# Regrouping the fp32 matrix work of a first stage: one place per row tile, the modulation a tile further ahead

## The chip, the cores and the metric

The kernel runs on one core of a Trainium2 chip. The metric is the device time of one launch in microseconds (us). Before the change it is 1366.4 us, the median of three runs (1366.26 to 1366.55).

The engines are TensorE (PE in the profile, its weight loads PEld), VectorE (DVE), ScalarE (ACT), GpSimd (POOL) and SyncE (SP, which here issues loads). Each works through its own instructions in order; between engines, semaphores make one wait for another.

## The reference

One layer of a hybrid decoder trunk over 1024 rows of 1024 numbers, all in float32. What matters here is its head:

```python
def rms_norm(x, w):
    xf = x.astype(jnp.float32)
    y = xf * lax.rsqrt(jnp.mean(xf * xf, axis=-1, keepdims=True) + EPS)
    return (y * w.astype(jnp.float32)).astype(x.dtype)

def hybrid_layer(x, c, ada_w, ada_b, norm_w, w_in, ...):
    mod = jax.nn.silu(c) @ ada_w + ada_b
    shift, scale, gate = jnp.split(mod, 3, axis=-1)
    h = rms_norm(x, norm_w) * (1 + scale[:, None, :]) + shift[:, None, :]
    proj = h @ w_in
    gm_u, gm_v, gm_z, ssm_z, xbc, dt_raw, g_a, g_b = jnp.split(proj, SPLITS, axis=-1)
    ...
    return x + gate[:, None, :] * (merged @ w_out)
```

The rest (a gated mixer over chunks, a state-space scan, two projections merged by gates, a last norm) follows the head and is not touched.

## The kernel before, in words

The first stage makes h, transposed so that its 1024 columns lie on the partitions, in eight row tiles of 128. It takes them in the order `KS = (0, 4, 1, 5, 2, 6, 3, 7)`; "tile n" below is the n-th in this order. Each tile has two halves of 512 columns (`halves(n)` says which comes first, a or b). What is done for a tile:

- `load_aw(n)`: SP loads the tile's part of `ada_w` (two transfers of 512 KB) into `aw`, which has two buffers; `load_w0(n)`: SP loads a slice of `w_in` into `w0r`.
- `matvec(n)`: eight fp32 matmuls, silu(c) times that part of `ada_w`, into `pm` (PSUM); ScalarE copies the result into `row`.
- `modulation_product(n)` ("the product"): two fp32 matmuls with a moving operand of one column, which sum the copied row over its four parts and turn it onto the partitions, in `pm` again.
- `modulation(n)`: two small instructions on VectorE that make the factors `md` from `pm`.
- `transposes(n, h)`: four fp32 matmuls against the identity, x to `px`.
- `rows_of_h(n, h)`: ScalarE writes h twice from `px` and `md`, once rounded to fp32r (the high part, such as `b22h`) and once in full (`hf`); VectorE makes the low part (such as `b22l`) as their difference.
- `split_w0(n)`: the same split into high and low for the weights.
- `first_products(n)`: twelve fp32r products into the accumulators `acc`: for each half, high times high, low weight times high, high weight times low.
- `dt_products(k)`: after every second tile, four fp32 matmuls of 32 columns into `pd`.
- `t_sum(k, i)` and `t_part(k, nm)`: four sums of h on VectorE (i from 0 to 3), and their splits on ScalarE and VectorE, for products by a Strassen-like scheme in later stages.

The order of all this on every engine is written by hand: `pin` keeps the instructions in the order of the program. The loop at the stage's end runs `first_products(n)`, a generator that gives way after each product, and puts the work for tile n+1 between the products of tile n: `prepare(n + 1)` says after which product, `between` adds the splits of the sums. In the stage after the first, TensorE runs the products `vx` and `vy`, whose weights SP loads into `av`.

Of the kernel before, what the change touches and what calls it, by code (L numbers as in the profile page):

```python
# [16 lines left out]
P = 128  # L17
D = 1024
S = 1024
KT = D // P  # L20
# [15 lines left out]
def hybrid_kernel(  # L36
# [7 lines left out]
    V, A, G, PE = nc.vector, nc.scalar, nc.gpsimd, nc.tensor  # L44
# [26 lines left out]
    def cst(shape, name, dt=F32):  # L71
        return const.tile(shape, dt, name=name, tag=name)
# [6 lines left out]
    pin = tc.keep_in_program_order  # L79

    def mm(acc, l, r, first=True, last=True):
        pin(PE.matmul(acc, l, r, start=first, stop=last))  # L82

    def tp(dst, src, idn):
        pin(PE.transpose(dst, src, idn))  # L85

    def f32(t):
        return t.bitcast(F32)

    def load(dst, src):  # L90
        pin(nc.sync.dma_start(dst, src))
# [6 lines left out]
    ones = cst([P, P], "ones")  # L98
# [16 lines left out]
    par = cst([P, P], "par")  # L115
# [27 lines left out]
    KS = (0, 4, 1, 5, 2, 6, 3, 7)  # L143
# [6 lines left out]
    def ax(name, tag="pm"):  # L150
        return psum0.tile([P, 512], F32, name=name, tag=tag, bufs=2 if tag == "px" else 1)
# [17 lines left out]
    def wide(name, dt=F32):  # L169
        return w4[0].tile([P, S], dt, name=name, tag="w4", bufs=w4[1])  # L170


    with tc.tile_pool(name="p0", bufs=1, reuse_waits="tile") as p0:
# [4 lines left out]
        accs = [[t[:, 0:512], t[:, 512:1024]] for t in accw]  # L178
        xt = [p0.tile([P, D], F32, name=f"x{t}", tag=f"x{t}") for t in range(NCH)]
        aw, wk = {}, {}  # L180
        pms, mds, hhs = {}, {}, {}

        def aw_tile(n):
            return p0.tile([P, KT, 2, P], F32, name=f"aw{n}", tag="aw", bufs=2)
# [56 lines left out]
        def warm(n):  # L241

            for _ in range(n):
                mm(pd[:, 0:P], ident, ones)

        tp(pp[:, 0:P], pk, ident)
        pin(V.tensor_copy(par, pp[:, 0:P]))
        warm(36)
        pin(V.tensor_scalar_add(par[:, 24:32], par[:, 24:32], 1.0))
        pin(A.activation(sc, par[:, 0:8], AF.Tanh, scale=0.5))  # L250
# [3 lines left out]

        def matvec(n):

            pms[n] = pm = ax(f"pm{n}")
            for i in range(KT):
                q = i % 4
                mm(pm[32 * q : 32 * q + 32, 0:256], scz[:, i, :], aw[n][:, i].rearrange("p j c -> p (j c)"),  # L260
                   i < 4, i >= 4)
            row = p0.tile([P, 256], F32, name=f"row{n}", tag="row", bufs=2)
            pin(A.copy(row, pm[:, 0:256]))
            mds[n] = row

        def modulation_product(n):

            pm, row = pms[n], mds[n]
            for j in range(2):
                mm(pm[:, 256 + j : 257 + j], row[:, j * P : (j + 1) * P], ones[:, 0:1])  # L270

        def modulation(n):

            k, pm = KS[n], pms[n]
            md = p0.tile([P, 2], F32, name=f"md{n}", tag="md", bufs=3)
            pin(V.tensor_add(md[:, 0:1], pm[:, 256:257], par[:, 16 + k : 17 + k]))
            pin(V.scalar_tensor_tensor(md[:, 1:2], pm[:, 257:258], par[:, 24 + k : 25 + k], par[:, 8 + k : 9 + k],
                                       op0=ALU.add, op1=ALU.mult))
            mds[n] = md

        def transposes(n, h):
            k = KS[n]
            px = pxs[n, h] if n + h == 0 else ax(f"px{n}_{h}", "px")
            for i in range(4):
                tp(px[:, i * P : (i + 1) * P], xt[4 * h + i][:, k * P : (k + 1) * P], ident)
            pxs[n, h] = px

        def rows_of_h(n, h):
            k, md, px = KS[n], mds[n], pxs[n, h]
            if k < 4 and h:  # L290
                b12 = wide(f"b12_{k}", F32R)
                hh, hl = b12[:, 0:512], b12[:, 512:1024]
            else:
                nm = ("b11" if k < 4 else ("b21", "b22")[h])
                hh, hl = bop[nm][0][k % 4], bop[nm][1][k % 4]
            if n + h:
                hfs[k, h] = hf_tile(k, h)
            hf = hfs[k, h]
            if n + h:
                for t in (hh, hf):  # L300
                    pin(A.activation(t, px, AF.Identity, scale=md[:, 1:2], bias=md[:, 0:1]))
            else:
                pin(V.tensor_scalar(hf, px, md[:, 1:2], md[:, 0:1], op0=ALU.mult, op1=ALU.add))
                pin(V.tensor_copy(hh, hf))
            pin(V.tensor_sub(hl, hf, f32(hh)))
            hhs[n, h] = (hh, hl)
# [6 lines left out]
        def t_sum(k, i):  # L313

            b11, b12, b21, b22 = (hfs[k + 4 * (j // 2), j % 2] for j in range(4))
            a, b, c = ((b11, b12, b11), (b12, b22, b12), (b22, b22, b11), (b21, b21, b22))[i]
            pin(V.tensor_sub(a, b, c))
# [53 lines left out]
        transposes(0, 0)  # L371
        split_w0(0)
        matvec(0)
        load_aw(2)
        load_w0(2)
        late_loads()
# [19 lines left out]
        rows_of_h(0, 1)  # L396
        warm(2)
        matvec(1)
        split_w0(1)
        for _ in range(2):  # L400
            next(start)
# [8 lines left out]
        def prepare(n):  # L410

            a, b = halves(n)
            k = (n - 2) // 2

            def second():
                modulation_product(n)
                transposes(n, b)
                if n % 2 == 0:
                    dt_products(k)
                modulation(n)  # L420
                if n % 2:
                    t_sum(k, 3)
                rows_of_h(n, a)
                if n % 2 == 0:
                    t_sum(k, 0)
                rows_of_h(n, b)
                if n % 2:
                    t_part(k, "t3")
                    t_part(k, "t2")
                else:  # L430
                    t_sum(k, 1)

            if n == 2:
                return {
                    4: lambda: (transposes(1, 1), rows_of_h(1, 1), matvec(n)),
                    8: lambda: (transposes(n, a), second()),
                }
            return {2: lambda: (matvec(n), transposes(n, a)), 7: second}

        def between(n, at):  # L440

            if n == KT - 1 and at == 6:
                dt_products(3)
            elif at == 2 and n > 1:
                k = (n - 2) // 2
                if n % 2:
                    t_part(k, "t4")
                else:
                    t_part(k, "t1")
                    t_sum(k, 2)  # L450

        for n in range(1, KT):
            todo = prepare(n + 1) if n + 1 < KT else {}
            for at, _ in enumerate(first_products(n), 1):
                if at == 1 and n + 2 < KT:
                    load_aw(n + 2)
# [5 lines left out]
                between(n, at)  # L462


    wpool = tc.tile_pool(name="wpool", bufs=1, reuse_waits="tile")
# [1107 lines left out]
    while tasks or work or posts:  # L1573
# [3 lines left out]
        while posts:  # L1577
            p, q, sq = posts.pop(0)
# [462 lines left out]
```

## Time and profile before

| | |
|---|---|
| median of three runs | 1366.4 us |
| time of the profiled execution | 1369.39 us |
| its span, first to last instruction | 1367.4 us |
| TensorE busy | 1352.4 us (99%) |
| VectorE busy | 1047.6 us (77%) |
| ScalarE busy | 799.6 us (58%) |
| GpSimd busy | 195.4 us (14%) |
| granted TensorE clock | 0.998 |
| first product of the stage after (`vx`) starts | 68.31 us |

The rows of a timeline give the start in us, the duration in us, the engine, the line, the operation, what is written from what, the shape, and how many instructions are taken together; in brackets stands the idle time of the engine before them and what ended it. Buffer numbers are left out there: `pm<-aw,scz` is a matvec, `pm<-ones,row` a product, `px<-ident,x` transposes, `pd<-hf,wd` dt products, `acc<-...` the first products. The profile counts an fp32 matmul as two instructions, except a transpose.

### The profile page before, as it was taken

To read this page: it belongs to the slowest core of one execution; us is meant where nothing else is said; L and a number is where in the kernel's file an instruction comes from. 1 tells how busy PE (TensorE), PEld (TensorE's weight loads), DVE (VectorE), ACT (ScalarE), POOL (GpSimd) and SP (SyncE) were. 2 spreads that over 40 slices of the span, in tenths; PEclk is the share of its full clock that TensorE was granted. 3 is DMA by queue.
4 is the path that set the end of the run, shared out by engine and by line. 5 is a ranking of instruction groups with operands and counts; after the bars stand their busy time and mean duration, and the time that the engine had idled before them with its cause. 6 is when DMAs were issued, how large, how long until landed. Compare 5 with 4: busy or idle time off the path is not lost.

```text
span 1367.4 us, 20180 instructions
## 1 busy us (share of the span) xinstructions
PE 1352.4 (99%) x6943; PEld 1117.4 (82%) x6943; DVE 1047.6 (77%) x1720; ACT 799.6 (58%) x1449; POOL 195.4 (14%) x191
## 2 busy tenths in 40 slices
PE   8999999999999999999999999999999999999997
PEld 7688888888888888888888888888888888888886
DVE  4786886777778898688887788457888866959976
ACT  5763666666656665465576665486877834233443
POOL 1000000000000000000000000016798971000002
PEclk9999999999999999999999999999999999999999
DMA  9675444343344657877665865488889958988913
GB/s 287 180 232 142 147 124 123 100 126 113 116 131 139 204 179 227 257 228 239 203 197 180 260 196 182 155 308 273 300 299 313 306 200 311 333 266 322 379 41 123
DMA packets 249530, 288.65 MB, mean 211 GB/s; under 512 B 16812, under 2 KB 196436, under 8 KB 249428
## 3 DMA queue, kind: packets, MB, share of 16 engines
q1 hardware_dynamic: 174868, 203.80, 46.9%
q10 hardware_dynamic: 74560, 83.57, 17.9%
q8 instruction: 55, 0.90, 0.3%
q14 instruction: 47, 0.39, 0.1%
HBM read 199.82 MB, written 87.49 MB: 210 GB/s over the span
## 4 chain that ended last, share of the span: by engine, by line
PE 90%; DVE 3%; DMA 3%; issue 1%; SPq 1%; ACT 1%; POOL 0%; POOLq 0%; DVEq 0%; ACTq 0%
PE xx L565 6%; PE xcb L565 6%; PE xz L565 6%; PE xuz L565 6%; PE xg L565 5%; PE pma L82 5%; PE ox L1885 3%; PE yuz L565 3%; PE yx L565 3%; PE ycb L565 3%; PE vx L970 3%; PE yp L1694 3%; PE yz L565 3%; PE yg L565 3%; PE yi L82 2%; PE sp L82 2%
## 5 line engine op out<-in xcount | busy, mean ns | idle before, releaser
L1139 POOL TENSOR_SCALAR_AFFINE_SELECT dcy<-dcy 128x1024 f32<-128x1024 f32 x32 | 37.7, 1179 | 788.0 <-DMA yl<-ya_d 744.6
L1147 ACT ACTIVATE dcy<-dcy,nacs 128x128 f32<-128x128 f32 x256 | 78.2, 389 | 4.9 <-POOL dcy L1139 4.2
L1163 DVE TENSOR_TENSOR dcy<-dcy,pc 128x1024 f32<-128x1024 f32 x32 | 39.0, 1220 | 9.0 <-PE pc L85 8.0
L1245 POOL TENSOR_TENSOR yz<-y,sl 128x512 f32<-128x512 f32 x32 | 44.3, 1386 | 2.5
L82 PE MATMUL pma<-yh,wah 128*128 128x512 f32 x128 | 43.1, 418 | 0.0
L82 PE MATMUL pma<-yh,wal 128*128 128x512 f32 x128 | 42.5, 413 | 0.0
L1040 ACT ACTIVATE ac<-ac 128x1024 f32<-128x1024 f32 x32 | 34.0, 1061 | 13.5 <-DVE ac L1038 13.3
L1170 ACT COPY bn<-pc 128x256 f32<-128x256 f32 x32 | 11.9, 372 | 49.8 <-DVE dcy L1163 49.8
L1632 DVE SCALAR_TENSOR_TENSOR yn<-yn,par,rb 128x512 f32<-128x512 f32 x32 | 25.2, 786 | 20.1 <-DMA yn<-yb_d 18.8
L82 PE MATMUL pma<-yl,wah 128*128 128x512 f32 x128 | 40.2, 395 | 0.0
L1135 ACT ACTIVATE ea<-dcy 64x512 f32<-64x512 f32 x64 | 39.8, 622 | 0.4
L1244 POOL TENSOR_TENSOR y<-y,ym 128x512 f32<-128x512 f32 (+1 forms) x32 | 37.0, 1156 | 3.5 <-DVE ym L1242 3.1
L1038 DVE SCALAR_TENSOR_TENSOR ac<-c2x,cwt,ac 128x1023 f32<-128x1023 f32 (+2 forms) x24 | 30.7, 1280 | 7.3 <-ACT ac L1036 7.2
L1038 DVE SCALAR_TENSOR_TENSOR ac<-c2cb,cwt,ac 128x1023 f32<-128x1023 f32 (+2 forms) x24 | 30.7, 1280 | 6.8 <-ACT ac L1036 6.6
L1242 DVE TENSOR_TENSOR ym<-yn,ea 128x512 f32<-128x512 f32 (+1 forms) x32 | 19.9, 623 | 19.9 <-PE yn L82 19.7
L82 PE MATMUL yi<-dcy,xd 128*64 128x128 f32 x512 | 35.0, 279 | 0.0
L82 PEld LDWEIGHTS yn<-sl,st 128*128 128x128 f32 x224 | 30.4, 195 | 5.3 <-POOL st L1208 2.8
L1900 POOL TENSOR_TENSOR r<-r,fnw 128x512 f32<-128x512 f32 x4 | 5.3, 1342 | 204.4 <-ACT junk L1898 204.4
L82 PE MATMUL yn<-sl,st 128*128 128x128 f32 x224 | 30.9, 278 | 2.4 <-POOL st L1208 2.4
L840 ACT CAST wbb<-wbr 128x512 fp32r<-128x512 f32 x32 | 19.8, 618 | 22.5 <-DMA wb_d<-wbb 18.9
L82 PE MATMUL sp<-xe,bn 128*128 128x256 f32 x112 | 32.7, 409 | 0.0
L1002 ACT ACTIVATE vm<-vm,vr 128x128 f32<-128x128 f32 x64 | 25.7, 483 | 11.3 <-DMA vm<-v_d 10.9
(2975 smaller groups left out, 4380.2 us busy)
## 6 DMA issues: line engine op xcount, KB each, us to landing
sl<-s_d SPq DMA_DIRECT2D x32, 768.0 KB, 6.7
s_d<-ac ACTq DMA_DIRECT2D x32, 512.0 KB, 3.6
wb_d<-wbb ACTq DMA_DIRECT2D x32, 512.0 KB, 3.6
dcy<-acs_d SPq DMA_DIRECT2D x32, 512.0 KB, 5.6
av<-in_w_in_dram SPq DMA_DIRECT2D x36, 256.0 KB, 3.2
aw<-in_ada_w_dram SPq DMA_DIRECT2D x16, 512.0 KB, 6.5
wbr<-in_w_proj_b_dram SPq DMA_DIRECT2D x32, 256.0 KB, 4.6
yb_d<-yz ACTq DMA_DIRECT2D x32, 256.0 KB, 6.0
```

Source lines behind the costliest of these rows:

```text
L82: pin(PE.matmul(acc, l, r, start=first, stop=last))
L565: pin(PE.matmul(ps, lw[:, k * P : (k + 1) * P], r[k], start=first and n + k == 0, stop=n == 2 and k == 3, skip_group_check=not first))
L970: pin(PE.matmul(ps[pn][j], l[:, j * P : (j + 1) * P], r, start=nm in ("p1", "p5", "p2") and n + units[i][1] == 0, stop=n == 2 and k == 3, ...
L1038: V.scalar_tensor_tensor(ac[:, s:], cc[:, : S - s], conv_wt[:, 3 - s, i : i + 1], ac[:, s:], op0=ALU.mult, op1=ALU.add)
L1135: link("A", lambda: A.activation(ea[hh * HD : (hh + 1) * HD], dcy.rearrange("p (j e) i l -> p e j (i l)", e=2)[hh * HD : (hh + 1) * HD, hh ...
L1139: link("G", lambda: G.affine_select(out=d8, in_=d8, compare_op=ALU.is_ge, fill=-1e30, base=0, pattern=[[0, 2 * HPG], [1, P]], channel_mult ...
L1147: link("A", lambda: A.activation(dcy[:, h, i, :], dcy[:, h, i, :], AF.Exp, bias=sub[:, i, h : h + 1]))
L1163: link("V", lambda: V.tensor_tensor(d3, d3, pc[:, 0:256].unsqueeze(1).to_broadcast([P, HPG, 256]), op=ALU.mult))
L1244: link("G", lambda: G.tensor_add(y1[:, :, t0:], y1[:, :, t0:], m[:, :, t0:]))
L1245: link("G", lambda: G.tensor_mul(yz, y1, sl[:, 4:6]))
L1694: pin(PE.matmul(ps[j], a[:, v, js], r, start=first and n + k == 0, stop=n == 2 and k == KT - 1, skip_group_check=not first))
L1885: pin(PE.matmul(ps, a[:, tsl], b[:, cs], start=first and n + j == 0, stop=n == 2 and j == 3, skip_group_check=not first))
```

## The change

Six edits, all in the first stage.

1. One PSUM tile `pm` serves all row tiles; its two halves of 256 columns take turns. Before, each row tile took a new `pm` from a pool with one buffer.
2. `matvec(n)` no longer copies its row; `row_of(n)` does, and is called on its own.
3. From tile 4 on there is one place per tile with fp32 matmuls among the products of the tile before, after its sixth product: the product of `pm`, both transposes, dt where it falls due, and the matvec of the tile after. Before there were two places: the matvec and the first transposes after the second product, the rest after the seventh.
4. So `matvec(n + 1)` stands in `prepare(n)`, for n = 3 to 6, ahead of `modulation(n)`. Tile 3 keeps its two places, and has the matvec of tile 4 added behind its second transposes.
5. `t_sum(k, 2)`, the third sum, moves behind `modulation(n)` in odd tiles.
6. `load_aw` for tiles 4 to 7 is called where the matvec before has freed its buffer (the table `AW`).

```diff
+        pm = ax("pm")
         def matvec(n):
-            pms[n] = pm = ax(f"pm{n}")
+            at = n % 2 * 256
             for i in range(KT):
                 q = i % 4
-                mm(pm[32 * q : 32 * q + 32, 0:256], scz[:, i, :], aw[n][:, i].rearrange("p j c -> p (j c)"),
+                mm(pm[32 * q : 32 * q + 32, at : at + 256], scz[:, i, :], aw[n][:, i].rearrange("p j c -> p (j c)"),
                    i < 4, i >= 4)
+        def row_of(n):
             row = p0.tile([P, 256], F32, name=f"row{n}", tag="row", bufs=2)
-            pin(A.copy(row, pm[:, 0:256]))
+            pin(A.copy(row, pm[:, n % 2 * 256 : n % 2 * 256 + 256]))
             mds[n] = row
...
             def second():
                 modulation_product(n)
+                if n > 3:
+                    transposes(n, a)
                 transposes(n, b)
                 if n % 2 == 0:
                     dt_products(k)
+                if 2 < n < KT - 1:
+                    matvec(n + 1)
                 modulation(n)
                 if n % 2:
+                    t_sum(k, 2)
                     t_sum(k, 3)
...
-            return {2: lambda: (matvec(n), transposes(n, a)), 7: second}
+            elif n == 3:
+                return {2: lambda: (matvec(n), row_of(n), transposes(n, a)), 7: second}
+            return {2: lambda: row_of(n), 6: second}
+        AW = {(1, 5): (4,), (2, 3): (5,), (2, 8): (6,), (3, 7): (7,)}
...
-                    t_sum(k, 2)
```

On TensorE, the products of tile 3 with the work for tile 4 (and, after the change, tile 5's matvec) among them. Before, from the second product of tile 3 to the eighth; of the transposes the first of each four is shown:

```order
L82 MATMUL acc1_231<-b22h1_187,w0h3_455 128x512
L82 MATMUL pm4_590<-aw4_520,scz_244 32x256 x8
L85 MATMUL px4_0_601<-ident_135,x0_232 128x128
...
L82 MATMUL acc0_230<-b22h1_187,w0l3_456 128x512
L82 MATMUL acc1_231<-b22h1_187,w0l3_456 128x512
L82 MATMUL acc0_230<-b22l1_191,w0h3_455 128x512
L82 MATMUL acc1_231<-b22l1_191,w0h3_455 128x512
L82 MATMUL acc0_230<-b21h1_203,w0h3_455 128x512
L82 MATMUL pm4_590<-ones_140,row4_599 128x1 x2
L85 MATMUL px4_1_617<-ident_135,x4_236 128x128
...
L82 MATMUL pd_229<-hf1_505,wd_270 32x512
...
L82 MATMUL acc1_231<-b21h1_203,w0h3_455 128x512
```

And now, the same stretch:

```order
L82 MATMUL acc1_231<-b22h1_187,w0h3_454 128x512
L82 MATMUL acc0_230<-b22h1_187,w0l3_455 128x512
L82 MATMUL acc1_231<-b22h1_187,w0l3_455 128x512
L82 MATMUL acc0_230<-b22l1_191,w0h3_454 128x512
L82 MATMUL acc1_231<-b22l1_191,w0h3_454 128x512
L82 MATMUL pm_273<-ones_140,row4_598 128x1 x2
L85 MATMUL px4_0_610<-ident_135,x0_232 128x128
...
L85 MATMUL px4_1_615<-ident_135,x4_236 128x128
...
L82 MATMUL pd_229<-hf1_506,wd_270 32x512
...
L82 MATMUL pm_273<-aw5_546,scz_244 32x256 x8
L82 MATMUL acc0_230<-b21h1_203,w0h3_454 128x512
```

The six products of the first half now follow each other, the product on `row4` comes one product sooner and without a matvec and four transposes ahead of it, and tile 5's matvec stands where tile 4's factors are made.

On VectorE, around the factors of tile 3. Before:

```order
L311 TENSOR_TENSOR t1l0_174<-hf0_241,t1h0_170 128x512
L317 TENSOR_TENSOR hf4_442<-hf4_442,hf0_241 128x512
L276 TENSOR_TENSOR md3_561<-pm3_528,par_146 128x1
L277 SCALAR_TENSOR_TENSOR md3_561<-pm3_528,par_146 128x1
L317 TENSOR_TENSOR hf4_442<-hf4_442 128x512
L305 TENSOR_TENSOR b22l1_191<-hf5_565,b22h1_187 128x512
```

And now:

```order
L315 TENSOR_TENSOR t1l0_174<-hf0_241,t1h0_170 128x512
L280 TENSOR_TENSOR md3_568<-pm_273,par_146 128x1
L281 SCALAR_TENSOR_TENSOR md3_568<-pm_273,par_146 128x1
L321 TENSOR_TENSOR hf4_441<-hf4_441,hf0_241 128x512
L321 TENSOR_TENSOR hf4_441<-hf4_441 128x512
L309 TENSOR_TENSOR b22l1_191<-hf5_573,b22h1_187 128x512
```

The third sum (`hf4<-hf4,hf0`) has moved from ahead of the factors to behind them. On ScalarE nothing moves: in both kernels the copy of `row4` stands behind tile 3's rows of h and the casts `t3h` and `t2h`.

The order doesn't show how far a wait reaches. In the built programs the factors wait on TensorE's semaphore for a count:

| factors of tile | before, count and the matmul that sets it | now |
|---|---|---|
| 3 | 160, its own product | 172, last matmul of matvec(4) |
| 4 | 190, its own product | 205, last matmul of matvec(5) |
| 5 | 224, its own product | 235, last matmul of matvec(6) |
| 6 | 254, its own product | 269, last matmul of matvec(7) |
| 7 | 288, its own product | 283, its own product |

On SP the loads of `aw6` and `aw7` now stand ahead of those of `w0r5` and `w0r6`.

More of the change, by code (lines that the diff above doesn't have):

```diff
@@ L180, in hybrid_kernel @@
         aw, wk = {}, {}
-        pms, mds, hhs = {}, {}, {}
+        mds, hhs = {}, {}
         def aw_tile(n):
@@ L373, in hybrid_kernel @@
         matvec(0)
+        row_of(0)
         load_aw(2)
@@ L398, in hybrid_kernel @@
         matvec(1)
+        row_of(1)
         split_w0(1)
@@ L434, in prepare @@
                 return {
-                    4: lambda: (transposes(1, 1), rows_of_h(1, 1), matvec(n)),
+                    4: lambda: (transposes(1, 1), rows_of_h(1, 1), matvec(n), row_of(n)),
                     8: lambda: (transposes(n, a), second()),
                 }
-            return {2: lambda: (matvec(n), transposes(n, a)), 7: second}
+            elif n == 3:
+                return {2: lambda: (matvec(n), row_of(n), transposes(n, a)), 7: second}
+            return {2: lambda: row_of(n), 6: second}
+        AW = {(1, 5): (4,), (2, 3): (5,), (2, 8): (6,), (3, 7): (7,)}
         def between(n, at):
@@ L454, in hybrid_kernel @@
             for at, _ in enumerate(first_products(n), 1):
+                if at == 1 and n == 1:
+                    load_aw(3)
                 if at == 1 and n + 2 < KT:
-                    load_aw(n + 2)
                     load_w0(n + 2)
@@ L462, in hybrid_kernel @@
                 between(n, at)
+                for i in AW.get((n, at), ()):
+                    load_aw(i)
     wpool = tc.tile_pool(name="wpool", bufs=1, reuse_waits="tile")
```

10 lines of the change are left out of this document (5 added, 5 removed).

## The prediction

> **What bounds the kernel now.** I read the profile's page first, then the busy time of each engine by stage, then the timelines of TensorE, ScalarE and VectorE through the first stage.
>
> ```profile
> span 1367.4 us, 20180 instructions
> PE 1352.4 (99%) x6943; PEld 1117.4 (82%) x6943; DVE 1047.6 (77%) x1720; ACT 799.6 (58%) x1449; POOL 195.4 (14%) x191
> ...
> PE 90%; DVE 3%; DMA 3%; issue 1%; SPq 1%; ACT 1%; POOL 0%; POOLq 0%; DVEq 0%; ACTq 0%
> ```
>
> TensorE is busy nearly always and holds 90% of the chain that ended last. The change touches the first stage alone, so what counts is what TensorE does there. By stage (span, then busy time of TensorE, weight loads, VectorE, ScalarE; the stretches are the products of row tiles 3, 4 and 7, and the stage after):
>
> ```profile
> 39.76:46.38 6.62, 6.62 (x49) 4.03 (x49) 3.75 (x9) 5.59 (x11) 0.00 (x0) 1.00 0.84 241
> 46.38:51.77 5.39, 5.37 (x41) 3.64 (x40) 4.98 (x10) 3.30 (x7) 0.00 (x0) 1.00 0.51 139
> 63.77:68.31 4.54, 4.34 (x20) 2.36 (x21) 3.25 (x6) 4.54 (x8) 0.00 (x0) 1.00 0.67 240
> 68.31:110.00 41.69, 41.69 (x185) 34.54 (x184) 29.77 (x50) 22.71 (x41) 0.00 (x0) 1.00 0.66 210
> ```
>
> TensorE is full, but ScalarE has 5.59 of 6.62 us beside tile 3 and VectorE 4.98 of 5.39 us beside tile 4: neither is far behind. The stage after has no gap (41.69 of 41.69 us), so what the first stage loses or gains reaches the end undiminished. TensorE, in order (start, duration):
>
> ```profile
> 40.42 1.07 PE L82 MATMUL pm<-aw,scz 128*32 128x256 f32 x16
> ...
> 42.84 0.39 PE L82 MATMUL acc<-b21h,w0h 128*128 128x512 f32 x1
> 43.07 0.60 PE L82 MATMUL pm<-ones,row 128*128 128x1 f32 x4
> 43.53 0.63 PE L85 MATMUL px<-ident,x 128*128 128x128 f32 x4
> 44.10 1.06 PE L82 MATMUL pd<-hf,wd 128*32 128x512 f32 x8
> 45.09 0.50 PE L82 MATMUL acc<-b21h,w0h 128*128 128x512 f32 x1
> ...
> 49.59 0.50 PE L82 MATMUL pm<-ones,row 128*128 128x1 f32 x4
> 49.95 0.64 PE L85 MATMUL px<-ident,x 128*128 128x128 f32 x4
> ...
> 51.12 0.62 PE L82 MATMUL acc<-b,w0h 128*128 128x512 f32 x2
> 51.77 0.73 PE L82 MATMUL acc<-b22h,w0h 128*128 128x512 f32 x2
> ```
>
> Two products take 0.46 us (0.62 of a pair less the overlap of its end; one is 0.23), so after 51.12 the next is due at 51.58. It starts at 51.77: 0.19 us lost to an operand, b22h, and the pair takes 0.73 in place of 0.62. That is the loss the new order goes after. ScalarE and VectorE around it:
>
> ```profile
> 38.92 0.78 ACT L301 ACTIVATE b22h<-px,md 128x512 fp32r<-128x512 f32 x1 [1.62 <-DVE md L277]
> ...
> 41.59 0.63 ACT L310 CAST t3h<-hf 128x512 fp32r<-128x512 f32 x1
> ...
> 42.62 0.39 ACT L263 COPY row<-pm 128x256 f32<-128x256 f32 x1
> ...
> 44.87 0.78 ACT L301 ACTIVATE b11h<-px,md 128x512 fp32r<-128x512 f32 x1 [1.03 <-DVE md L277]
> ...
> 46.87 0.78 ACT L301 ACTIVATE hf<-px,md 128x512 f32<-128x512 f32 x1
> ...
> 50.94 0.78 ACT L301 ACTIVATE b22h<-px,md 128x512 fp32r<-128x512 f32 x1 [1.62 <-DVE md L277]
> ...
> 56.88 0.78 ACT L301 ACTIVATE b11h<-px,md 128x512 fp32r<-128x512 f32 x1 [1.03 <-DVE md L277]
> ...
> 62.94 0.78 ACT L301 ACTIVATE b22h<-px,md 128x512 fp32r<-128x512 f32 x1 [1.62 <-DVE md L277]
> ```
>
> ScalarE starts the rows of h for tile n when VectorE has the factors md(n); b22h ends at 51.72 and TensorE starts at 51.77. And tile 4's row copy, queued behind four activations and two casts, ends at 43.01, when its product starts (43.07). Of the row copies the view of that tile says:
>
> ```profile
>   PEld pm L82: 0.5, 2
> ```
>
> So twice TensorE already had to wait for row (tiles 4 and 6). ScalarE's queue is just in time at two places.
>
> **Where the change puts the wait.** The product now stands after six products of tile n, not after matvec, four transposes and seven: it is wanted earlier. The row copy has not moved on ScalarE. And md(n) for n = 3 to 6 now waits, by the program's semaphores, for the last matmul of matvec(n+1), since both are in the one tile pm; before it waited for its own product. Behind the waiting product on TensorE stand its transposes, dt, matvec and all products that follow; behind the waiting md on VectorE stand the sums and the low parts of h, and ScalarE's four rows of h wait for it. That closes a ring: rows of h (ScalarE), row copy, product, eight transposes, dt, matvec (TensorE), md (VectorE), rows of h of the next tile. It is run once per tile, and I cost it link by link. Missing links:
>
> ```profile
> 28.41 0.60 PE L85 MATMUL px<-ident,x 128*128 128x128 f32 x4
> 28.94 1.07 PE L82 MATMUL pm<-aw,scz 128*32 128x256 f32 x16
> ...
> 34.92 1.07 PE L82 MATMUL pm<-aw,scz 128*32 128x256 f32 x16
> ...
> 37.94 0.64 PE L85 MATMUL px<-ident,x 128*128 128x128 f32 x4
> ```
>
> ```profile
> 32.40 0.78 ACT L301 ACTIVATE b11h<-px,md 128x512 fp32r<-128x512 f32 x1 [1.64 <-DVE md L277]
> 36.11 0.37 ACT L263 COPY row<-pm 128x256 f32<-128x256 f32 x1 [0.92 <-PE pm L82]
> ```
>
> ```profile
> 32.02 0.16 DVE L276 TENSOR_TENSOR md<-pm,par 128x1 f32<-128x1 f32 x1 [0.80 <-PE pm L82]
> ...
> 49.96 0.68 DVE L317 TENSOR_TENSOR hf<-hf,hf 128x512 f32<-128x512 f32 x1
> ```
>
> From the end of a matvec (34.92 + 1.07 = 35.99) to its reader (36.11) is 0.12 us; from md to the first row of h, 32.02 to 32.40, is 0.38.
>
> *Odd tiles (3 and 5).* Rows of h, casts and row copy to product: 38.92 to 43.07, 4.15 us, in unchanged order. Product to transposes: 43.07 to 43.53, 0.46. Transposes: 0.57 to pd for four (43.53 to 44.10), four more at 0.11 (28.41 to 28.94 is 0.53 for four with a changeover of 0.09) make 1.01. pd 44.10 to 45.09, 0.99. matvec 1.07, then 0.12 and 0.38. Sum 8.18 us, where 38.92 to 44.87 was 5.95 and 50.94 to 56.88 was 5.94: +2.23 and +2.24.
>
> *Even tile 4.* Four rows of h at 0.67 (44.87 to 46.87 is three), the row copy's 0.38 and 0.06 to the product make 3.11. Then 0.36 (49.59 to 49.95), transposes 0.53 + 0.44, matvec 1.07, and 0.50. Sum 6.01, where 44.87 to 50.94 was 6.07: -0.06.
>
> *Tile 6.* It has no matvec behind it; there VectorE is last. In tile 4 the third sum at 49.96 stood 5.09 after 44.87, and md7 now stands in that sum's place in the same row of work: 5.09 and 0.38 make 5.47 us, where 56.88 to 62.94 was 6.06: -0.59.
>
> *Tile 3's own start.* Its factors wait for matvec(4), now behind the transposes at 37.94: 37.94 + 0.53 + 1.07 + 0.50 = 40.04, where 38.92 was: +1.12.
>
> Together 1.12 + 2.23 - 0.06 + 2.24 - 0.59 = 4.94 us. From tile 7's first row of h on, the order is as before. TensorE's own work per tile is shorter than the ring (6.62 and 5.39 us before, with the same instructions), so the ring sets the pace. Two links could only be shorter than taken. pd is followed by matvec, which no row of before shows; the nearest row is pd to products, 0.99 as taken, and without a changeover (0.09 at the transposes) the two odd tiles would give back 0.2. And in tile 6 the row copy no longer waits for a matvec, which may let VectorE's work run 0.1 sooner. I take 4.8, towards the plain sum because its links are measured whole.
>
> *The third sum behind md* frees 0.6 us of VectorE (49.96 to md5's former place) ahead of md3 and md5. Both now wait for the ring: 6.01 in tile 4 against VectorE's 5.47, so it is worth nothing there. At md7 it counts, and is in the 5.47. Behind md the two sums take 1.2 us; the low part b22l needs ScalarE's hf, which ends 0.38 + 0.67 + 0.78 after md starts, so the sums don't delay it: nothing.
>
> *The loads.* On SP, aw6 and aw7 go ahead of w0r5 and w0r6, and all wait for a buffer that a matvec frees.
>
> ```profile
> 30.07 1.16 SPq L91 DMA_DIRECT2D aw<-in_ada_w_dram  x2
> ...
> 36.05 1.37 SPq L91 DMA_DIRECT2D aw<-in_ada_w_dram  x2
> ...
> aw<-in_ada_w_dram SPq DMA_DIRECT2D x16, 512.0 KB, 6.5
> ```
>
> aw4 is issued by 31.23, lands by 37.7 at the median 6.5 us, and is wanted at 37.94 + 0.53 = 38.47: 0.7 us to spare. aw5, freed at 36.05, lands by 43.9 and is wanted at 40.04 + 4.15 + 0.46 + 1.01 + 0.99 = 46.65. w0r5 is held past matvec(4) and wanted when tile 4's casts run, some 10 us later: nothing.
>
> [...] The trace shows no VectorE read of pm while a matvec writes it: md reads at 32.02, and the next matvec starts at 34.92. [...]
>
> **Rivals.** *Independent halves.* If md(n) waits only for its own product, matvec no longer lies in the ring. Odd tiles then need 4.15 + 0.46 + 0.50, about 5.1 us, under TensorE's 6.6; the late b22h vanishes three times (tiles 3, 5, 7: 0.19 + 0.11 each, 0.90), and in tile 7 this too:
>
> ```profile
> 65.17 0.73 PE L82 MATMUL acc<-b22l,w0h 128*128 128x512 f32 x2 [0.20 <-DVE b22l L305]
> ```
>
> 0.20 + 0.11 more: -1.2 us, 1365.2, not slower. It decides if md3 starts before matvec(4) ends. Against it stands the semaphore's count; for it, that the sums and the regrouping then pay as written. Chance 0.08.
>
> *Given back later.* A later wait of TensorE could shrink by what comes late:
>
> ```profile
> PE yn L82 <- POOL st L1208: 2.4, 1, 2.4
> PE x0p L1694 <- DVE p6bl L1670: 0.3, 1, 0.3
> ```
>
> If all 2.4 us vanished, +2.4 would be left: 1368.8. Against it: that wait is for GpSimd's work on data of this same program, which shifts along. (VectorE's p6bl also moves one place ahead, at most 0.3 us.) Chance 0.05.
>
> *A late load.* aw4 has 0.7 us to spare; landing 2 us late it would add about 1.3, 1372.5, and more if aw5 and aw6 follow. For it, 6.5 us is a median over loads that ran under different traffic; against it, aw5 has 2.7 us to spare and the later ones more. Chance 0.04.
>
> **How the numbers follow.** The profiled execution took 1369.39 us (span 1367.4), 3.0 over the median of the runs, 1366.4. Added to it, 4.8 gives 1374.2; for the median, 1371.2. The ring's chance is 0.83. It has some 25 links in four rounds; if each were off by 0.04 us the same way, that is 1 us. The range goes a little further up for the late load and further down towards the rival that gives back: 1369.6 to 1372.6. A measurement of this kernel can tell 0.2%, 2.7 us. Ring and late load lie beyond it: slower 0.87. The other two lie within: same 0.12, and 0.01 for faster.
>
> **What would show it.** After: VectorE idle for one to two us before md3, md4 and md6, released by pm. TensorE waits for row about 1.35 us in tiles 3 and 5: 4.15 against 2.8, which is hf's end (0.67 + 0.78), b22l (0.7) and two products (0.57) with the hand-overs. In tiles 4 and 6 it waits about 0.3 (3.11 against 2.8). It waits for the low part of h about 0.35 in each tile, since the first products no longer have a matvec and transposes among them. Further, tile 3's products some 8.2 us apart from tile 4's; the first vx at about 73.1 instead of 68.3. It is wrong if md3 starts right behind its product, if the row copies come before TensorE wants them, or if the first vx is late by 4.8 and the end is not.

## The result, and the profile after

The changed kernel takes 1373.74 us, the median of six runs (1371.9 to 1377.38), against 1366.43 us for the kernel before, run beside it. The ratio is 1.0061 [1.0050, 1.0071]: slower by 6.8 to 9.7 us. The prediction had 1371.2 us and a range up to 1372.6; it is right in direction and in the first stage, and 2.5 us short at the end, outside its range.

The page of the changed kernel's profiled execution (1371.9 us):

```profile
span 1370.0 us, 20170 instructions
PE 1353.2 (99%) x6943; PEld 1116.9 (82%) x6943; DVE 1047.1 (76%) x1720; ACT 800.5 (58%) x1449; POOL 192.9 (14%) x191
...
PE 86%; DMA 4%; DVE 3%; POOL 3%; ACT 2%; issue 1%; SPq 0%; POOLq 0%; DVEq 0%; ACTq 0%
```

Shares hardly differ. The first stage does. TensorE, from the row tile whose factors are the first to wait (start, duration):

```profile
34.60 0.63 PE L82 MATMUL acc<-b11h,w0h 128*128 128x512 f32 x2
...
41.09 0.74 PE L82 MATMUL acc<-b22h,w0h 128*128 128x512 f32 x2
...
42.48 0.73 PE L82 MATMUL acc<-b22l,w0h 128*128 128x512 f32 x2 [0.19 <-DVE b22l L309]
44.39 0.61 PE L82 MATMUL pm<-ones,row 128*128 128x1 f32 x4 [1.17 <-ACT row L267]
44.86 1.07 PE L85 MATMUL px<-ident,x 128*128 128x128 f32 x8
45.86 1.07 PE L82 MATMUL pd<-hf,wd 128*32 128x512 f32 x8
46.75 1.05 PE L82 MATMUL pm<-aw,scz 128*32 128x256 f32 x16
...
49.41 0.73 PE L82 MATMUL acc<-b11h,w0h 128*128 128x512 f32 x2
...
58.80 0.61 PE L82 MATMUL pm<-ones,row 128*128 128x1 f32 x4 [1.18 <-ACT row L267]
...
73.35 0.62 PE L987 MATMUL vx<-p1v0h,b11h 128*128 128x512 f32 x2
```

Ahead of the product on `row4` TensorE stands idle 1.17 us until ScalarE's copy ends, then transposes, dt and tile 5's matvec run behind it, and only after the matvec do the factors come. ScalarE and VectorE in the same stretch:

```profile
40.26 0.78 ACT L305 ACTIVATE b22h<-px,md 128x512 fp32r<-128x512 f32 x1 [2.71 <-DVE md L281]
...
43.95 0.39 ACT L267 COPY row<-pm 128x256 f32<-128x256 f32 x1
48.58 0.78 ACT L305 ACTIVATE b11h<-px,md 128x512 fp32r<-128x512 f32 x1 [3.41 <-DVE md L281]
...
54.66 0.78 ACT L305 ACTIVATE b22h<-px,md 128x512 fp32r<-128x512 f32 x1 [2.22 <-DVE md L281]
...
62.64 0.78 ACT L305 ACTIVATE b11h<-px,md 128x512 fp32r<-128x512 f32 x1 [3.07 <-DVE md L281]
...
67.98 0.78 ACT L305 ACTIVATE b22h<-px,md 128x512 fp32r<-128x512 f32 x1 [1.47 <-DVE md L281]
```

```profile
47.86 0.16 DVE L280 TENSOR_TENSOR md<-pm,par 128x1 f32<-128x1 f32 x1 [1.95 <-PE pm L82]
```

The matvec ends at 46.75 + 1.05 = 47.80, the factors start at 47.86, the rows of h at 48.58: the ring of the prediction, closed. The waits of TensorE (in total, times, longest), without the one at the start and those of 0.3 us:

```profile
PE pm L82 <- ACT row L267: 2.3, 2, 1.2
PE xx L582 <- ACT c1x L598: 0.7, 1, 0.7
PE acc L82 <- DVE b22l L309: 0.6, 3, 0.2
...
PE acc L82 <- DVE b11l L309: 0.4, 2, 0.2
```

The wait for `c1x`, near 357 us, was not in the profile of before.

In the profile of before stood another thing that the prediction missed. Its wait of 2.4 us for `st`, which ends at 928.4 us, has a sequel (stretch, busy times; the third number from the end is TensorE's granted clock):

```profile
928.46:931.87 3.41, 3.41 (x16) 3.41 (x17) 1.02 (x2) 1.14 (x2) 2.80 (x3) 0.50 0.91 324
```

For 3.41 us behind the pause TensorE ran at half its clock (granted 0.50). This is part of why that execution took 3.0 us more than the median of its kernel: the second profile of before, below, has the same pause without such a stretch, and takes 1.7 us less from the first `vx` to the last product (1290.76 against 1292.48).

### The profile page after: what moved, and what is told of

It is laid out like the page before. It is cut to its first block, busy times and chain, and to the rows that moved or that the text cites. A ratio compares the mean times of both kernels' runs of the same rounds, so it can differ in the third digit from the quotient of the medians.

```text
span 1370.0 us, 20170 instructions
## 1 busy us (share of the span) xinstructions
PE 1353.2 (99%) x6943; PEld 1116.9 (82%) x6943; DVE 1047.1 (76%) x1720; ACT 800.5 (58%) x1449; POOL 192.9 (14%) x191
## 4 chain that ended last, share of the span: by engine, by line
PE 86%; DMA 4%; DVE 3%; POOL 3%; ACT 2%; issue 1%; SPq 0%; POOLq 0%; DVEq 0%; ACTq 0%
PE xz L582 6%; PE xx L582 6%; PE xcb L582 6%; PE xuz L582 6%; PE xg L582 6%; PE pma L82 5%; PE ox L1902 3%; PE ycb L582 3%; PE vx L987 3%; PE yp L1711 3%; PE yz L582 3%; PE yx L582 3%; PE yuz L582 3%; PE yg L582 3%; PE zz L582 2%; PE zx L582 2%
## 5 line engine op out<-in xcount | busy, mean ns | idle before, releaser
L1262 POOL TENSOR_TENSOR yz<-y,sl 128x512 f32<-128x512 f32 x32 | 43.9, 1370 | 2.5
L82 PEld LDWEIGHTS yi<-dcy,xd 128*64 128x64 f32 x512 | 27.3, 136 | 5.7 <-issue 3.1
```

The lines of the kernel that those rows point to most:

```text
L1262: link("G", lambda: G.tensor_mul(yz, y1, sl[:, 4:6]))
```

## The experiments

**A yardstick.** The start of `vx` moves with chance events ahead of tile 2, such as half-clock stretches of the start. So I take the time from the first product of tile 2 (34.36 us before, 34.60 after) to the first `vx`: 33.95 us before (34.36 to 68.31) and 38.75 after (34.60 to 73.35). The other profiles:

| kernel | tile 2 to first `vx`, us, each profile | ratio to the kernel before, run beside it |
|---|---|---|
| before | 33.95, 33.91, 33.92 | |
| changed | 38.75, 40.39, 40.39, 38.77 | 1.0061, 1.0071, 1.0055, 1.0063 |
| changed, factors first | 32.82 | 1.0014 |
| changed, row early | 36.72 | 1.0015 |
| changed, both | 37.88 | 1.0034 |
| changed, pauses filled | 38.77, 38.75 | 1.0041, 1.0038 |
| before, third sum alone | 32.71, 32.70 | 0.9997, 0.9999 |

### The two kernels again

> The changed kernel once more, unaltered, for a second profile and more times. In the first profile the first vx started at 73.35 us against 68.31 before, 5.04 late, but the span was only 2.6 longer and the median of the runs 7.3. Theory 1 (the ring in the first stage is the whole lasting loss; what comes on top or is given back is chance in later waits): vx again at 73.1 to 73.6 us, TensorE waiting twice about 1.2 us for row, and later waits of TensorE that differ from the first profile's in place and size. Theory 2 (the later program reacts to the shift in a fixed way): the same later waits again, 0.7 us for c1x near 357 us among them.

> The kernel before, unaltered, for a second profile. In its first one TensorE waited 2.4 us for st at 928 us, behind one GpSimd instruction that took 3.51 us in place of 1.09, and ran the next three us at half pace. If that was chance, it isn't there again, the first vx is at 68.1 to 68.6 us and the span some 4 us shorter than 1367.4. If it belongs to the kernel, it is there again.

The changed kernel came to 1375.98 us (1371.62 to 1380.89), ratio 1.0071 [1.0054, 1.0088]; the kernel before to 1367.63 in a single run, 1366.12 in the median of the 17 beside the others. So the changed kernel does not only lie higher, it scatters over 9 us. The kernel before again waited 2.4 us for `st`, without the half clock behind it. The changed kernel's profiled run, at 1380.89, has the wait for `c1x` again (1.1 us), and its first `vx` at 78.71 us, where 73.1 to 73.6 was expected. It shows what the scatter is made of. TensorE behind the second wait for row, and the granted clock:

```profile
62.51 0.61 PE L82 MATMUL pm<-ones,row 128*128 128x1 f32 x4 [1.18 <-ACT row L267]
62.98 1.75 PE L85 MATMUL px<-ident,x 128*128 128x128 f32 x8
64.66 1.94 PE L82 MATMUL pd<-hf,wd 128*32 128x512 f32 x8
```

```profile
22.25:25.67 3.42, 2.03 (x17) 1.25 (x20) 2.61 (x7) 0.75 (x2) 0.76 (x2) 1.00 0.92 259
25.67:32.49 6.82, 6.82 (x32) 4.73 (x25) 3.22 (x8) 3.31 (x7) 0.00 (x0) 0.50 0.92 242
59.80:63.21 3.41, 2.06 (x11) 1.18 (x10) 2.71 (x5) 3.41 (x8) 0.00 (x0) 1.00 0.08 29
63.21:66.63 3.42, 3.42 (x20) 1.72 (x22) 0.81 (x2) 0.08 (x1) 0.00 (x0) 0.50 0.00 0
```

```profile
940.44:943.85 3.41, 3.41 (x17) 3.31 (x17) 1.99 (x3) 0.97 (x3) 2.65 (x3) 0.50 0.79 271
```

Transposes and dt take 1.75 and 1.94 us where they took 1.07: the clock is 0.50 from 63.21 for 3.41 us. The starts 25.67, 63.21 and 940.44 lie 37.54 and 877.23 us apart, 11 and 257 times 3.413 us, so in this profile the stretches sit on a grid, whose steps I call cells. In the cells ahead of the first two, TensorE was idle 1.39 us (3.42 less 2.03) and 1.35; the third follows a wait of 2.4 us for `st`. The 1.35 us were two pauses, of 0.18 and 1.18. A pause of 1.17 us thus costs its own length and can cost another 1.64 us: 40.39 less 38.75.

It does not always. In the first profile the second pause for row lies whole in a cell (cells of the same length, counted back from the half clock at that execution's end, which starts at 1367.83 us), and the clock stays full behind it:

```profile
57.11:60.52 3.41, 2.23 (x18) 1.53 (x21) 2.83 (x5) 2.46 (x6) 0.00 (x0) 1.00 0.00 0
60.52:63.94 3.42, 3.42 (x32) 1.99 (x25) 0.28 (x2) 1.30 (x2) 0.00 (x0) 1.00 0.14 29
```

In the changed kernel's first stage, the two cells that were followed by half clock held the pause for row together with the wait for the low part of h (1.35 and 1.38 us idle); those with the pause nearly alone (1.18 to 1.24) were not. But idle time in the cell isn't the whole rule: at the start a cell with 1.24 us idle was followed by half clock (row early, below) and one with 1.42 was not (the third sum alone). What else decides stays open.

### The ring without the matvec in it

```diff
                 if n % 2 == 0:
                     dt_products(k)
+                modulation(n)
                 if 2 < n < KT - 1:
                     matvec(n + 1)
-                modulation(n)
```

> The changed kernel with modulation(n) ahead of matvec(n+1) in the order, so that md(n) waits for its own product alone and the matvec waits for md; nothing else differs. If the wait of md for the matvec makes the ring (theory 1), the first vx comes at about 67.1 us (1.2 ahead of before's 68.31) and the time is 0.5 to 2 us under before. If the ring closes over the late row copy alone (rival: ScalarE's queue is what is full), most of the loss stays and vx comes after 70 us.

```profile
67.50 0.62 PE L987 MATMUL vx<-p1v0h,b11h 128*128 128x512 f32 x2
```

The first `vx` comes at 67.50, after 32.82 us from tile 2, 5.93 less than in the changed kernel and 1.1 less than before. No wait for row is left. That shows the ring: only the place of the factors moved, and the whole loss of the first stage went. The median, 1367.85, is still not below the kernel before, where 0.5 to 2 us under it was expected: 1.0014 [1.0005, 1.0022]. Its waits:

```profile
PE xx L582 <- ACT c1x L598: 1.2, 1, 1.2
PE pm L82 <- DMA aw<-in_ada_w_dram: 1.0, 2, 0.9
...
PE x0p L1711 <- DVE p6bl L1687: 0.7, 2, 0.4
```

The wait for `c1x` alone takes back the 1.1 us that the first stage gained. The wait of 0.9 us for `aw` lies inside the first stage: in this version, which runs ahead of the changed kernel, a load does come late.

### A pure delay

```diff
                     todo[at]()
+                if at == 12 and n == KT - 1:
+                    idle = ax("idle")
+                    for _ in range(20):
+                        mm(idle[:, 0:P], ident, ones)
```

> The kernel before with 20 dummy fp32 matmuls of 128 columns behind the first stage's last product: about 5.0 us of TensorE's time and nothing else, a pure shift of all that follows. If the later program just shifts (theory 1), the time is 5 us (4.5 to 5.5) over before. If it reacts to a shift of this size (theory 2), the time is some 7 us over before, as in the changed kernel.

```profile
72.60 0.70 PE L974 MATMUL vx<-p1v0h,b11h 128*128 128x512 f32 x2
```

Into the kernel before, this puts 4.36 us of idle work ahead of `vx` (72.60 against 68.24 in the second profile of before; 5.0 was expected) and no pause. The ratio is 1.0049 [1.0034, 1.0064], 4.6 to 8.7 us. Nothing of a delay is given back, then, which settles that rival of the prediction. (The one profile alone would mislead: it happens to have no wait for `st`.) The interval even begins a little above 4.36: the medians lie 5.8 us apart, so something of the surplus over the first stage seems to come without any pause. What, no run here shows.

### The pauses filled

```diff
             def second():
+                if n in (4, 6):
+                    pxs[n, a] = ax(f"px{n}_{a}", "px")
+                    for _ in range(5):
+                        mm(pxs[n, a][:, 0:P], ident, ones)
                 modulation_product(n)
```

(`transposes` then takes the `px` that is there.)

> The changed kernel with five idle fp32 matmuls (0.215 us each) on TensorE ahead of the products of tiles 4 and 6, where it waits 1.17 us for row; nothing else moves. Ring: the first vx stays at 73.3 to 73.6, since row comes no sooner. Clock theory (the surplus over the 5.0 us comes from half-clock stretches of 3.41 us that TensorE's pauses set off): no granted clock of 0.5 between 35 and 75 us, median 1371.3 to 1372.6, and hardly a run above 1374. Rival, later stages react badly to the late start: the same median and spread as the changed kernel, 1374 to 1376.

> The changed kernel once more, on the same chip as the filled one. Both theories: 1373.5 to 1376. Clock theory: runs spread over 3 us or more, and the profiled run has its first vx at 73.4 plus 1.7 us for each half-clock stretch ahead of it.

> The changed kernel again. Both theories: 6 to 10 us over the kernel before. Clock theory: from tile 2's first product to vx 38.75 us, or 40.4 with a half-clock stretch behind a pause for row. If the wait for c1x belongs to this kernel, 0.7 to 1.1 us of it near 357 us.

> The changed kernel with its pauses for row filled, again. Clock theory: 38.75 us from tile 2's first product to vx, never 40.4; the median 1 to 3 us under the changed kernel on the same chip. Rival: the same median as the changed kernel. The wait for c1x: absent if the first filled profile was typical.

> The kernel before, for its profile and its spread beside the others: 33.9 us from tile 2's first product to vx, no half-clock stretch in it, wait for c1x 0 to 0.4; ratio to the kernel before 1.000 within 0.001.

Twice the changed and the filled kernel ran side by side on one chip: 1376.84 and 1374.31 us (ratios 1.0055 [1.0040, 1.0071] and 1.0041 [1.0026, 1.0056]), then 1373.48 and 1371.65 (1.0063 [1.0047, 1.0079] and 1.0038 [1.0025, 1.0051]). Filled is lower by 2.5 and 1.8 us in the medians, though the intervals overlap. The kernel before, taken once more, came to 1.0001 [0.9992, 1.0010]. The profiles are clearer. The changed kernel, then the filled one:

```profile
41.35:44.77 3.42, 2.04 (x11) 1.13 (x10) 2.53 (x5) 3.42 (x8) 0.00 (x0) 1.00 0.93 271
44.77:48.18 3.41, 3.41 (x17) 1.86 (x21) 1.00 (x3) 0.25 (x1) 0.00 (x0) 0.50 0.23 69
```

```profile
43.03 1.28 PE L82 MATMUL px<-ones,ident 128*128 128x128 f32 x10
44.37 0.61 PE L82 MATMUL pm<-ones,row 128*128 128x1 f32 x4
```

With the filling, the product on `row4` starts at 44.37, without it at 44.39, and the first `vx` comes at 73.34: the ring doesn't care what TensorE does while it waits. In five profiles of kernels that pause for row (the four of the table and one more below) a half-clock stretch followed a pause twice; in three profiles of filled ones none did. These are few, but the clock averaged over a run is on record for every run; one stretch of 3.41 us at half clock lowers it by 0.0012 (half of 3.41 in some 1370 us). Its mean over the runs, beside that of the kernel before on the same chip, is:

| kernel (runs) | its clock | the kernel before | estimated cost of the difference, us |
|---|---|---|---|
| changed (6, 6, 6) | 0.9973, 0.9972, 0.9980 | 0.9988, 0.9981, 0.9987 | 1.9, 1.2, 1.0 |
| filled (6, 5) | 0.9978, 0.9988 | 0.9981, 0.9987 | 0.3, -0.1 |

(The cost is an estimate, at 1.64 us per stretch.) So the changed kernel loses some 1 to 2 us more to half clock than the kernel before, and the filled one next to nothing more. The filling also took away the wait for `c1x`, which I had not expected to hang on it; that is explained below. So the difference of about 2 us is not the clock's alone. In the first set the filled median missed the clock theory's 1371.3 to 1372.6, in the second it met it.

### The third cell: the pause near 928 us

Twelve idle fp32 matmuls ahead of the first products `yn` that read `st`, in the kernel before, the changed and the filled one:

```diff
             yn = bank(f"yn{self.g}_{s}")
+            if (self.g, s) == order[0]:
+                for _ in range(12):
+                    mm(yn[:, 0:P], ident, ones)
```

> The kernel before with twelve idle fp32 matmuls (2.6 us) on TensorE near 928 us, ahead of the products yn that wait 2.4 us for st in most executions. They take the pause away and with it the half-clock stretch behind it. Clock theory: no granted clock of 0.5 behind 928 us; an execution that had the pause ends about where it did without the 1.7 us of the half clock, one that had none ends 2.6 us later: median within 1.5 us of the kernel before, spread narrower than its 5 to 6 us. Rival, the spread has another cause: spread unchanged.

> The changed kernel with the same twelve idle matmuls near 928 us. Its pauses for row in the first stage stay. Clock theory: half-clock stretches in the first stage only, in some executions: 5.5 to 8 us over the same version of the kernel before, the runs spread over 2 to 4 us in steps of about 1.7. Rival, later stages react to the late start: as far over it as the filled version.

> The changed kernel with the pauses for row filled by ten idle matmuls and the one near 928 us by twelve. Clock theory: no half-clock stretch between 35 us and the end; 5.0 to 5.8 us over the same version of the kernel before (5.0 of the first stage, some tenths at c1x), narrow spread, and 0.5 to 3 us under the version that keeps the pauses for row. Rival: no difference between these two.

This missed. The half clock behind 928 us was gone, but all three kernels got a new wait of 4.5 to 5.0 us that ends between 1135 and 1142 us, and half clock behind or at the end of it (in the kernel before 0.50 from 1135.33 to 1138.74 us). There:

```profile
PE x3p L1697 <- DVE tha L1509: 5.0, 1, 5.0
```

They took 1377.53, 1381.94 and 1380.89 us, where the unpadded kernel before took 1367.48. The filled version lies 1.1 us under the unfilled, within the scatter (1379.9 to 1383.01 against 1379.11 to 1384.42). Nothing on the size of the clock's part follows; why VectorE's `tha` came late I did not pursue.

### Row early, and both

```diff
                 if 2 < n < KT - 1:
                     matvec(n + 1)
+                    row_of(n + 1)
...
-            return {2: lambda: row_of(n), 6: second}
+            return {6: second}
```

> The changed kernel with the copy of row n+1 directly behind matvec(n+1), ahead of the rows of h on ScalarE. Ring theory: the product no longer waits for row, md still waits for matvec; the ring keeps 1.12 us of tile 3's start and 0.88 in tiles 3 and 5 (2.8 + 0.46 + 1.01 + 0.99 + 1.07 + 0.50 = 6.83 against 5.95), less 0.37 and 0.59 in tiles 4 and 6: first vx at 70.2. Clock theory: no pause over 0.4 us, so 1368.0 to 1369.3 and a narrow spread. Rival, later stages react to any late start: 1370 to 1372.

> Factors ahead of matvec(n+1), and the row copy directly behind matvec(n+1): no ring at all and no wait for row. Ring theory: first vx at 67.5 or a little earlier, TensorE without a wait for row or low part over 0.2 us. Clock theory: 1365.5 to 1367, about the kernel before or up to 0.8 below it, less if the wait for c1x near 350 us (1.2 us in the version with the factors alone) stays. Rival, later stages lose for another reason tied to the new order of loads: 1367.5 to 1369.

Row early: tile 2 to `vx` is 36.72 us, 2.79 over before where 1.92 was expected. The wait for row is gone as the ring said, and the rest of the ring stays. Of TensorE's waits between 36 and 74 us:

```profile
PE acc L82 <- ACT b22h L305: 0.9, 2, 0.5
```

The even tile, which I had at 5.70 us, takes 6.07, and tile 3 starts later, since the row copy now holds up its rows of h. The ratio is 1.0015 [1.0005, 1.0025], about 2 us. Its profile has a half-clock stretch from 24.65 to 28.06 us (0.50), behind the pauses of the start, so such stretches are not bound to pauses for row.

Both together missed: 37.88 us and 1.0034 [1.0022, 1.0046]; the first `vx` came at 72.76 us and not at 67.5. TensorE's waits in the first stage tell the cause:

```profile
PE pm L82 <- DVE md L281: 2.4, 3, 1.1
```

With the row copy of tile n+1 ahead of tile n's rows of h on ScalarE, those rows wait for matvec(n+1); and matvec(n+1), which writes the one `pm`, waits for the factors of tile n to be read. The ring had closed again by another link.

### The third sum alone

```diff
                 if n % 2:
+                    t_sum(k, 2)
                     t_sum(k, 3)
...
-                    t_sum(k, 2)
```

> The kernel before with the third sum behind the factors, nothing else of the change. VectorE reaches md3, md5 and md7 0.6 us sooner, up to where their products on TensorE set it. The late b22h (0.19 + 0.11 us at tiles 3, 5 and 7) goes, and the late b22l of tile 7 (0.31) perhaps: first vx 0.6 to 1.2 us earlier, and the median 0.5 to 1.2 us under the kernel before, if nothing later takes it back. Rival: the later stages' waits move by as much the other way, no difference.

> The third sum behind the factors alone, again: 32.7 us from tile 2's first product to vx, 1.2 less than before. If that reaches the end, the median is 0.5 to 1.5 us under the kernel before and the lowest runs 1.2 under its lowest; if the later waits take it back, no difference.

In the kernel before, this edit alone gives 32.71 and 32.70 us from tile 2 to `vx`: 1.22 less, what the prediction had for the three late `b22h` and tile 7's late `b22l`. The medians don't move: 0.9997 [0.9983, 1.0010] and 0.9999 [0.9990, 1.0008]. In the second profile `vx` is at 66.84 us, against 69.11 in the profile of before taken beside it, and the last product of both ends at 1357.8 us. The lead of 2.3 us, 3.0 behind the wait for `st` (925.34 against 928.32), went between 1131 and 1189 us. Less than half of it stands in waits that this profile of before does not have, the rest in steps that no listed wait explains:

```profile
PE x0p L1694 <- DVE p6bl L1670: 0.7, 2, 0.4
PE x0p L1694 <- DVE p1bl L1670: 0.6, 1, 0.6
```

```profile
1140.00:1190.00 50.00, 49.22 (x214) 39.60 (x213) 37.83 (x60) 15.80 (x28) 1.14 (x1) 1.00 0.96 356
```

There the DMA engines are busy 96% and VectorE stands just in time. That a transfer-bound stretch swallows an earlier start fits both rows; no run took the load away, so it is argued, not shown. Nor do the intervals by themselves rule out a gain of 1.2 us (0.0009 of the time). No version tried is shown to beat the kernel before.

## Why the prediction was wrong, point by point

**The ring: right, link by link.** Rows of h started at 40.26, 48.58, 54.66, 62.64 and 67.98 us. The steps are 8.32, 6.08, 7.98 and 5.34, forecast 8.18, 6.01, 8.18 and 5.47. From tile 2 on the stage takes 4.80 us more, forecast 4.8. That it agrees to a hundredth is partly luck, since two steps came out longer (by 0.14 and 0.07) and two shorter (by 0.20 and 0.13). The link that was furthest off is the one from the factors to the first row of h in tile 4: 0.72 us (47.86 to 48.58), taken as 0.38. The first `vx` came at 73.35 and not 73.1, because tile 2 was already 0.24 late. The waits for row were 1.17 and 1.18 us, forecast 1.35, the low parts of h 0.2 and not 0.35. In tiles 4 and 6 the product came some 0.3 late, as forecast (the trace has the first at 51.67 us, where the two products from 50.80 us on, at 0.57, would have let it start at 51.37). Putting the factors ahead of the matvec took all of it away. The loads came in time: from tile 2 to `vx` no wait for `aw` stands in the profile.

**"What the first stage loses or gains reaches the end undiminished": the step that failed.** On its strength the prediction added 4.8 us to 1366.4, and put everything behind the first stage and all changes of the clock at nothing. For losses the sentence held as a floor: the delay arrived whole. But it took every stretch of TensorE at its own length, and left out what a pause does to the work behind it and what a shift does to waits further on. The four profiles of the changed kernel have a mean span of 1373.1 us, the three of before 1365.8. The 7.3 us between them divide so:

| part | us |
|---|---|
| the ring | 4.82 |
| half-clock stretches behind the pauses for row (1.64 us each, in two of four profiles) | 0.82 |
| ahead of tile 2 | 0.86 |
| behind the first `vx` | 0.76 |

The 0.86 is one profile's 6.83 us of half clock at the start. I put it down to chance, but that isn't settled: such a stretch stands in two of the eleven profiles with the new order of loads, and in none of the seven with the old. The 0.76 is a balance: the wait for `c1x` is 0.8 longer (1.0 on average, against 0.2 before), the wait for `st` 0.9 shorter (1.2 against 2.1), the half clock behind that wait costs 0.3 more, and 0.6 comes after 1126 us, from a cause that stays open. So the two parts that the runs tie to the change are the half clock behind its pauses, by the table of clocks 1 to 2 us with all its stretches counted, and the wait for `c1x`, 0.8 us. The medians of the changed kernel lie 7.3 to 9.9 us above those of the kernel before, and what is left of that is open; the delay, which came to 5.8 for 4.36, suggests that a part of it needs no pause. For gains the sentence isn't borne out either: 1.22 us of the third sum could not be found at the end.

**The range** went up only by 1 us for link errors and a little for a late load. Half clock and the wait for `c1x` both add to the time, and the range had no term for either. The half clock stood in the profile of before, behind the pause near 928 us, and would have priced a new pause.

**The rivals.** Independent halves: no, the factors did wait for the matvec. Given back later: no, the delay reached the end. Late load: no.

## What to carry to other kernels

When work is regrouped, follow the ring of waits through all engines once around; its links, taken from rows of the old trace, gave each row tile's step here to within 0.2 us. Then price each new pause of TensorE twice, by its own length and by the chance of a half-clock stretch behind it (here 1.64 us, behind a pause for row in two of five profiles), and look for such stretches in the trace you start from. A loss ahead of a full stage arrived whole here, or with a surplus, and a gain was not found again, so look for the next stretch where another engine or the transfers are just in time.

## What the runs showed of the hardware

**A packet of the queue `instruction` seems to delay a store.** The wait for `c1x` comes through VectorE from the loads of `ag` (in the changed kernel VectorE's `gacc` waits 2.22 us for `ag`, ScalarE's `c1x` 3.04 for `gacc`, TensorE 0.72 for `c1x`). SP issues these loads when the store `s_d<-ac` ahead of them has landed (its queue waits 10.3 us for that, 9.4 before). The store's traffic in the changed and the filled kernel, in 40 slices of 346.5 to 352 and of 346.5 to 351 us, with the queues below:

```profile
GB/s 0 0 0 0 0 0 0 0 0 0 0 119 0 0 0 119 320 335 328 328 328 335 343 343 343 335 201 37 30 22 22 22 22 0 0 0 0 0 0 0
...
q10 hardware_dynamic: 528, 0.52, 28.8%
q8 instruction: 1, 0.02, 1.4%
```

```profile
GB/s 0 0 0 0 0 0 0 0 0 0 0 0 0 0 0 0 0 73 355 355 337 328 373 346 346 355 328 364 337 337 319 110 0 0 0 0 0 0 0 0
...
q10 hardware_dynamic: 528, 0.52, 34.1%
```

In the changed kernel a packet of `q8 instruction` falls into the store, which ends in a tail at 22 GB/s. The packet takes 1.2 us (1.4% of 16 engines over 5.5 us); the whole execution has 55 of them, with 0.90 MB. In the profile of before ag's issue follows the store's by 3.24 us (342.30 to 345.54, the packet at 342.14), in the first of the changed kernel by 4.06 (347.44 to 351.50, the packet at 348.10). Over 18 profiles it is 3.23 to 3.25 us where no such packet starts behind the store's issue (nine profiles, the three filled ones among them), 3.7 where one starts 0.2 to 0.4 us behind it, 4.06 to 5.17 where it starts 0.5 to 2.7 us behind, which is so in all five profiles of kernels that pause for row and in the factors-first one. No run moved the packet and nothing else, so the cause is argued from these 18. The packet does not fall at the same time in each program: with the ten idle matmuls it starts 3 to 5 us sooner (348.10 and 349.44 us in the first and fourth profile of the changed kernel, 345.04 and 344.68 in the filled ones). On this reading edits cost or gain far from where they stand: the wait for `c1x` is 0.7 to 1.1 us in the profiles of the changed kernel, and the filled ones have none.

**Near 920 us GpSimd or VectorE took longer where the two ran at once.** The 2.4 us for `st` seem to come from this. Before, then after:

```profile
916.50 3.51 POOL L1139 TENSOR_SCALAR_AFFINE_SELECT dcy<-dcy 128x1024 f32<-128x1024 f32 x1 [18.63 <-ACT ea L1135]
916.57 2.50 DVE L1378 TENSOR_TENSOR yl<-yl,yh 128x512 fp32r<-128x512 f32 x4
```

```profile
922.24 1.09 POOL L1156 TENSOR_SCALAR_AFFINE_SELECT dcy<-dcy 128x1024 f32<-128x1024 f32 x1 [18.62 <-ACT ea L1152]
922.32 1.55 DVE L1395 TENSOR_TENSOR yl<-yl,yh 128x512 fp32r<-128x512 f32 x1
```

In the first, GpSimd's instruction takes 3.51 us, 2.42 more than the median of the 32 of its line (1.09), about the length of VectorE's run of four (2.50). In the third profile of the changed kernel, which has the wait of 2.4 us too, it takes 3.52. In the second of the two stretches VectorE's takes 1.55 in place of 0.69 and TensorE does not wait. In both GpSimd's record starts first, by 0.07 or 0.08 us, so the order of the starts doesn't tell which of the two takes longer; what does, no run shows. Of the four profiles of the changed kernel two have a wait of 2.4 us for `st` and two none, the three of before have 2.4, 2.4 and 1.4: this belongs to the scatter more than to the change.
